# A decoder step on one core: fp32r products whose moving columns come in turn from two halves

## The chip, the core and the metric

The kernel runs on one core of a Trainium2 chip. The metric is the device time of one execution in microseconds (us), lower is better. Five engines matter: TensorE (PE in the profile; PEld is its weight load), VectorE (DVE), ScalarE (ACT), GpSimd (POOL) and SyncE (SP), which issues most transfers. Products are written into PSUM; only DVE and ACT read PSUM here.

## What is computed

One layer of a hybrid decoder trunk and a final norm, for a prompt of 1024 tokens and 8 sample tokens that share the weights. In the reference, cut to what matters:

```python
def layer(x, ...):
    h = rmsnorm(x, g_mix)
    u = h @ w_in                                  # 1024 -> 512 (pool) + 512 (value) + 512 (gate)
    glu = val * sigmoid(gate)
    ya = pool_mixer(concat(pool_hist, a), ...)    # windows 2/4/8/16, per-group 128x128 map
    yb = conv_mixer(concat(conv_hist, glu), ...)  # depthwise conv of width 31, LayerNorm, swish
    x = x + concat(ya, yb) @ w_out
    x = x + cross_attn(rmsnorm(x, g_attn), mk, mv, w_q, w_o)   # 4 heads, 256 memory tokens
    h = rmsnorm(x, g_ffn)
    x = x + (silu(h @ w_gate) * (h @ w_up)) @ w_down           # 2816 hidden channels
    return x

y = rmsnorm(layer(x), g_final)
```

The memory's keys and values (`mem_kv`) and the new pool and conv states are outputs too.

## The kernel before

**Layout.** Channels lie on the 128 partitions, tokens along the free dimension: T = 1032 columns, first the 512 even prompt tokens, then the 512 odd ones, then the 8 samples. Each product of an fp32 weight and an fp32 activation is made of three fp32r products: both factors are split into a rounded part and a rest, and `PASSES` gives the three pairs (rounded x rounded, rounded x rest, rest x rounded). All accumulate into the same PSUM columns. For every such matmul a 128x128 weight tile is loaded, and the moving operand is a contiguous run of columns: 344 (a third of T, `CW`) for the projections, 256 for keys and scores, 512 for values and attention outputs, 512 or 260 (half of 520, `TW`) in the gated and down parts. Before the change moving columns are read in the order in which they lie, and written to PSUM in the same order.

**Readers of PSUM.** DVE and ACT read a finished product once or twice: to scale it, add it to a residual, take an exponential, or split it again. Helpers `ch3`, `halves` and `as_banks` bring the SBUF side into the shape of the PSUM side (three banks of 344, two of 260).

**Stages,** in order of time: input projection with conv and pool windows (up to about 180 us), memory keys and values, output projection (to 297), queries, scores, softmax and attention values, mixed with the sample tokens' own attention, which DVE sums from caches that arrive by transfer (297 to 449), attention's output projection (449 to 540), then the gated part (22 hidden tiles, 540 to about 970; each from tile 2 on is `seven(f)`: seven products in the manner of Strassen and Winograd over blocks A11, A12, A22, S1 to S4), the down projection (`down(u)`, to 1138) and its last tiles with the final norm (`last_down`, `final`).

**What sets the order.** The body of the kernel only lists tasks: `add({"PE": pe(CW, 9)}, emit, reads, writes)`. `Program.order` plays them through as a list scheduler, with a price in us for each engine that may take the task, and emits each engine's instructions in the order that this play gives; where two engines are allowed ("DVE" or "Pool"), the one that would end sooner gets it. `pe(n, count)` is the price of `count` fp32r matmuls of `n` columns. The prices set the order and the engine alone; on the chip semaphores decide when a task runs.

Of the kernel before, what the change touches and what calls it, by code (L numbers as in the profile page):

```python
# [10 lines left out]
AF = mybir.ActivationFunctionType  # L11
# [250 lines left out]
def hybrid_step_kernel(ctx: ExitStack, tc: tile.TileContext, io):  # L262
# [228 lines left out]
    def step3(ps, w, wkeys, cols, x, k, first, last, spans=range(NCH), keys=None):  # L491


        def emit(e):
            for p, (wi, xi) in enumerate(PASSES):
                for c in spans:
                    e.matmul(ps[:, c, :CW], w[:, wi, cols], x[:, xi, c * CW : (c + 1) * CW],  # L497
                             start=first and p == 0, stop=last and p == 2)
# [234 lines left out]
    def gate_out(j, ps):  # L733
        t = scr(f"t{j}")
        tk = (t,)
        if j == 0:
            add({"ACT": act(T, True)}, lambda e: e.activation(ch3(t[:]), ps[:, :, :CW], AF.Copy), all3(ps), [tk])
# [7 lines left out]
    def value_out(j, ps, t):  # L745
# [4 lines left out]
        if j == 0:  # L750
            add({"DVE": dve(T), "ACT": act(T, True)}, lambda e: (
                e.activation(ch3(gb[:, i]), ps[:, :, :CW], AF.Copy) if e is nc.scalar else
                e.tensor_copy(ch3(gb[:, i]), ps[:, :, :CW])), all3(ps), [gk])
            add({"DVE": dve(T), "Pool": pool_tt(T)}, lambda e: e.tensor_tensor(gb[:, i], gb[:, i], t[:], ALU.mult), [gk, (t,)], [gk], lock=True)
        else:
            add({"DVE": dve(T)}, lambda e: e.tensor_tensor(ch3(gb[:, i]), ps[:, :, :CW], ch3(t[:]), ALU.mult), all3(ps) + [(t,)], [gk])
# [102 lines left out]
    def mixer_in(g):  # L859
        ps = group("w_in", xop)  # L860
        ab, ai = a2[g // 2], g % 2
        add({"DVE": dve(T)}, lambda e: e.tensor_tensor(ch3(ab[:, ai]), ps[:, :, :CW], ch3(Rx[:]), ALU.mult), all3(ps) + RX, [(ab, ai)])
# [6 lines left out]
    def keys(q):  # L869
        ps = mm_buf(f"kps{q}", 1)  # L870
        for i in range(2):
            w, wkeys = w_take("w_k")
            for k in range(KT):
                def emit(e, k=k, i=i, w=w):
                    for p, (wi, xi) in enumerate(PASSES):
                        e.matmul(ps[:, 0, i * NMEM : (i + 1) * NMEM], w[:, wi, block_cols(k)], memg[k // 4][:, xi, k % 4],  # L876
# [4 lines left out]
            kf[:], ps[:, 0].rearrange("p (i m) -> p i m", i=2), Rm().unsqueeze(1).to_broadcast([P, 2, NMEM]), ALU.mult),  # L881
# [62 lines left out]
    def values(c):  # L944
        ps = mm_buf(f"vps{c}", 2)
        for kk in range(4):
            w, wkeys = w_take("w_v")
            for k in (2 * kk, 2 * kk + 1):
                def emit(e, k=k, w=w):
                    col = (k % 2) * 512  # L950
                    for p, (wi, xi) in enumerate(PASSES):
                        for m in range(2):
                            e.matmul(ps[:, m], memg[k // 4][:, xi, k % 4, m * P : (m + 1) * P], w[:, wi, col : col + 512],  # L953
# [3 lines left out]
        for m in range(2):  # L957
            add({"ACT": act(512, True, 1)}, lambda e, m=m: e.activation(
                vf[:, m], ps[:, m], AF.Copy, scale=rmc[:, 2 * m : 2 * m + 1]), [(ps,), ("rmc",)], [(vf, m)])
# [7 lines left out]
    def out_a(n):  # L967
# [8 lines left out]
        add({"DVE": dve(T)}, lambda e: e.tensor_tensor(ch3(x1[j][:, i]), ps[:, :, :CW], ch3(x1[j][:, i]), ALU.add),  # L976
# [6 lines left out]
    def out_b(n):  # L983
# [8 lines left out]
        add({"DVE": dve(T)}, lambda e: e.tensor_tensor(ch3(x1[j][:, i]), ps[:, :, :CW], ch3(x1[j][:, i]), ALU.add), all3(ps) + [xk], [xk])  # L992
# [886 lines left out]
```

## Time and profile before

| | |
|---|---|
| median of 3 runs | 1219.57 us (1217.78 to 1220.19) |
| span of the profiled execution | 1217.6 us |
| TensorE busy | 1202.0 us, 99% of the span, 7736 matmul records |
| weight loads (PEld) busy | 1125.9 us, 92% |
| DVE, ACT, POOL busy | 931.2, 524.8, 250.1 us |
| mean granted TensorE clock | 0.997 |

The page lists no other time for the profiled execution than its span; it is set against the median of the runs here. TensorE is busy nearly throughout, but "busy" says only that some matmul was in flight: what one matmul takes has to be read from runs of equal matmuls that follow each other without a wait. A row of the lines by form gives line, engine, operation, output and inputs, shape, count, then busy us, mean ns of one from its start to its end (which is more than its distance to the next, since matmuls overlap), and idle time before it.

### The profile page before, as it was taken

What the parts mean: (1) busy time and instruction counts of PE and PEld (TensorE: products, weight loads), DVE (VectorE), ACT (ScalarE), POOL (GpSimd) and SP (SyncE); (2) the same over time, 40 slices, a digit from 0 to 9 for tenths busy, and PEclk for the clock granted to TensorE, in tenths of its full rate; (3) what the DMA queues carried; (4) which work ended last, traced back from release to release, by engine and by line L of the source; (5) the groups of instructions that cost most, each with busy time, mean ns of one, the idle gap of its engine ahead of it and who ended that gap; (6) DMA issues with size and microseconds to landing.
All of it is one profiled execution on the core that took longest, in us unless ns stands there. A gap on an engine that the chain in (4) does not pass through costs nothing.

```text
span 1217.6 us, 19433 instructions
## 1 busy us (share of the span) xinstructions
PE 1202.0 (99%) x7736; PEld 1125.9 (92%) x7736; DVE 931.2 (76%) x1548; ACT 524.8 (43%) x718; POOL 250.1 (21%) x297
## 2 busy tenths in 40 slices
PE   9999999999999999999999999999999999999997
PEld 9999988999999979999999999999999999999886
DVE  7899999766258886679877787777867798879754
ACT  7765656455135633454222322233222355544533
POOL 3568842231110102131000000000000024332101
PEclk9999999999999999999999999999999999999998
DMA  7334676326386774421332233222313597678612
GB/s 289 82 77 111 145 213 214 125 105 205 112 263 202 238 272 156 122 87 62 122 113 80 96 114 108 109 80 97 123 70 105 207 310 210 180 185 224 149 51 89
DMA packets 60170, 179.69 MB, mean 148 GB/s; under 512 B 7792, under 2 KB 11568, under 8 KB 58800
## 3 DMA queue, kind: packets, MB, share of 16 engines
q1 hardware_dynamic: 53392, 157.56, 37.1%
q0 software_dynamic: 6256, 20.54, 9.7%
q8 instruction: 60, 0.98, 0.3%
q10 hardware_dynamic: 432, 0.36, 0.1%
q14 instruction: 30, 0.25, 0.1%
HBM read 144.66 MB, written 33.78 MB: 147 GB/s over the span
## 4 chain that ended last, share of the span: by engine, by line
PE 78%; DVE 4%; DMA 1%; issue 1%; ACT 0%; POOL 0%; DVEq 0%; SPq 0%; POOLq 0%; ACTq 0%
PE pr L1355 47%; PE po L497 7%; PE fd L1698 6%; PE ps L497 5%; PE oa L497 4%; PE ob L497 4%; PE sc L1052 1%; DVE spcache_k L1149 1%; PE vps L953 1%; PE pv L1110 1%; DMA sbcache_v<-pd 1%; PE kps L876 0%; PE pmap L896 0%; DMA spcache_k<-in_cache_k 0%; DMA pd<-prow 0%
## 5 line engine op out<-in xcount | busy, mean ns | idle before, releaser
L1355 PEld LDWEIGHTS pr<-ab,wTb 128*128 128x128 f32 x1056 | 131.8, 188 | 3.5
L1355 PE MATMUL pr<-ab,wTa 128*128 128x260 f32 x1056 | 133.6, 282 | 0.2 <-DVE su L1371 0.2
L1355 PE MATMUL pr<-ab,wTb 128*128 128x260 f32 x1056 | 133.0, 282 | 0.0
L1355 PEld LDWEIGHTS pr<-ab,wTa 128*128 128x128 f32 x1056 | 130.8, 188 | 2.4 <-DVE su L1371 0.4
L1355 PE MATMUL pr<-ab,wG 128*128 128x512 f32 x528 | 129.2, 393 | 0.0
L1371 DVE TENSOR_TENSOR su<-pr,su 128x520 f32<-128x520 f32 (+1 forms) x112 | 77.7, 695 | 57.6 <-PE pr L1355 57.4
L1355 PEld LDWEIGHTS pr<-ab,wG 128*128 128x128 f32 x528 | 96.3, 188 | 19.7 <-DVE wG L396 0.4
L497 PE MATMUL ps<-xop,w 128*128 128x344 f32 x720 | 114.1, 320 | 0.0
L497 PEld LDWEIGHTS ps<-xop,w 128*128 128x128 f32 x720 | 113.6, 188 | 0.0
L1355 PEld LDWEIGHTS pr<-hb,dV 128*128 128x128 f32 x768 | 98.8, 188 | 4.1
L1355 PE MATMUL pr<-hb,dV 128*128 128x260 f32 x768 | 100.1, 283 | 0.0
L497 PE MATMUL ps<-xq,w 128*128 128x344 f32 x576 | 94.9, 322 | 0.1
L497 PEld LDWEIGHTS po<-oo,w 128*128 128x128 f32 x576 | 90.8, 188 | 0.6 <-DVE oo L1115 0.4
L497 PE MATMUL po<-oo,w 128*128 128x344 f32 x576 | 91.3, 320 | 0.0
L497 PEld LDWEIGHTS ps<-xq,w 128*128 128x128 f32 x576 | 90.8, 188 | 0.4 <-DMA w<-in_w_q 0.4
L710 DVE SCALAR_TENSOR_TENSOR cacc<-glu,vec,cacc 128x511 f32<-128x511 f32 (+14 forms) x116 | 76.9, 740 | 0.0
L1355 PE MATMUL pr<-hb,dW 128*128 128x512 f32 x288 | 74.5, 394 | 0.1
L385 ACT ACTIVATE w<-raw 128x1024 fp32r<-128x1024 f32 (+1 forms) x37 | 35.0, 950 | 86.7 <-PE po L497 24.4
L1698 PE MATMUL fd<-ho,w 128*128 128x260 f32 (+1 forms) x432 | 69.1, 321 | 0.0
L1698 PEld LDWEIGHTS fd<-ho,w 128*128 128x128 f32 x432 | 62.0, 188 | 6.9 <-issue 0.5
L1382 POOL MEMSET su<- 128x16 f32 x22 | 2.5, 113 | 318.9 <-PE pr L1355 267.7
L1355 PE MATMUL pr<-ab,wU 128*128 128x512 f32 x264 | 64.6, 393 | 0.0
(311 smaller groups left out, 2195.7 us busy)
## 6 DMA issues: line engine op xcount, KB each, us to landing
gr<-in_w_gu SPq DMA_DIRECT2D x44, 512.0 KB, 3.4
hb<-su SPq DMA_DIRECT2D x8, 1040.0 KB, 4.6
hs<-hb SPq DMA_DIRECT2D x16, 520.0 KB, 5.3
dr<-in_w_dn SPq DMA_DIRECT2D x16, 512.0 KB, 4.4
spcache_k<-in_cache_k SPq DMA_DIRECT2D x12, 512.0 KB, 5.7
hs<-hb SPq DMA_DIRECT2D x12, 512.0 KB, 4.6
raw<-in_w_in SPq DMA_DIRECT2D x10, 512.0 KB, 3.3
hb<-he SPq DMA_DIRECT2D x8, 520.0 KB, 2.8
```

Of the source, the lines that this page charges most:

```text
L385: e.activation(dst(0), src(), AF.Copy, scale=1.0 if gain is None else gain)
L497: e.matmul(ps[:, c, :CW], w[:, wi, cols], x[:, xi, c * CW : (c + 1) * CW], start=first and p == 0, stop=last and p == 2)
L710: e.scalar_tensor_tensor(acc[h][:, n:], src[:, : HALF - n], w, acc[h][:, n:], ALU.mult, ALU.add)
L953: e.matmul(ps[:, m], memg[k // 4][:, xi, k % 4, m * P : (m + 1) * P], w[:, wi, col : col + 512], start=(k == 0 and p == 0), stop=(k == KT ...
L1052: e.matmul(bank()[:, i * NMEM : (i + 1) * NMEM], qop[2 * h + dt][:, qi, tt * P : (tt + 1) * P], kk[:, ki, 2 * (h % 2) + dt], start=(dt == ...
L1110: e.matmul(ps[:, c], v[:, vi, m, col : col + P], pT[h][m][:, pi, sl], start=(m == 0 and p == 0), stop=(m == 1 and p == 2))
L1149: e.scalar_tensor_tensor(piece[:, b], piece[:, b], 1.0, bc[:, b], ALU.mult, ALU.mult, accum_out=out(m)[:, first + b : first + b + 1])
L1355: e.matmul(bank(c), w[:, wi, cols(j)], xs[0](j, xi)[:, c * n : (c + 1) * n], start=onto is None and j == 0 and p == 0, stop=j == nj - 1 an ...
L1371: from_sums(sums, "DVE", dve, lambda e, src, sl: e.tensor_tensor(as_banks(o(sl), src), src, as_banks(a(sl), src), op), [akey], [okey])
L1382: add({"Pool": 0.12}, lambda e: e.memset(o(), 0.0), [], keys)
L1698: e.matmul(view(i), w[:, wi, col : col + P], hops[k][:, xi, half, lo - half * HALF + i * width // count : lo - half * HALF + (i + 1) * wid ...
```

## The change

Three things change together.

1. Every fp32r matmul reads its moving columns in turn from two halves of the run: with n columns, first column 0, then n/2, then 1, then n/2 + 1 (`turns`). The output is written to PSUM in that order, one column after the other (`placed` only gives it the same shape). So PSUM column 2i holds column i of the first half and column 2i + 1 column i of the second. Plain fp32 products and transposes keep their order.
2. Every reader of such a PSUM result takes every second column (`drawn`): first the even places, then the odd ones, and writes or pairs them with contiguous SBUF halves. The shapes gain a dimension of 2; the number of elements stays. The maximum over a row of scores needs no order and is left as it is.
3. The planner's price of a matmul, `pe`, goes from 0.0135 + 0.000417 n us to the larger of 0.1125 and 0.0027 + 0.000417 n. For 260, 344 and 512 columns that is 0.1219 to 0.1125, 0.1570 to 0.1461 and 0.2270 to 0.2162 us.

```diff
+    def turns(ap):
+        return ap.rearrange("p (h n) -> p n h", h=2)
+    def placed(ap):
+        return ap.rearrange("p (n h) -> p n h", h=2)
+    def drawn(ap):
+        return ap.rearrange("p (n h) -> p h n" if len(ap.shape) == 2 else "p c (n h) -> p c h n", h=2)
+    def drawn3(ps):
+        return drawn(ps[:, :, :CW])
+    def ch3h(ap):
+        return ap.rearrange("p (c h n) -> p c h n", c=NCH, h=2)
...
     def pe(n, count=1):
-        return (0.0135 + 0.000417 * n) * count
+        return max(0.1125, 0.0027 + 0.000417 * n) * count
...
-                    e.matmul(ps[:, c, :CW], w[:, wi, cols], x[:, xi, c * CW : (c + 1) * CW],
+                    e.matmul(placed(ps[:, c, :CW]), w[:, wi, cols], turns(x[:, xi, c * CW : (c + 1) * CW]),
...
-            add({"DVE": dve(T)}, lambda e: e.tensor_tensor(ch3(t[:]), ps[:, :, :CW], ch3(Rx[:]), ALU.mult), all3(ps) + RX, [tk])
+            add({"DVE": dve(T)}, lambda e: e.tensor_tensor(ch3h(t[:]), drawn3(ps), ch3h(Rx[:]), ALU.mult), all3(ps) + RX, [tk])
...
-                e.activation(pr[:, tt], bank()[:, i * NMEM : (i + 1) * NMEM], AF.Exp, bias=st[:, 2 + i : 3 + i],
+                e.activation(halves(pr[:, tt]), drawn(bank()[:, i * NMEM : (i + 1) * NMEM]), AF.Exp, bias=st[:, 2 + i : 3 + i],
...
     def as_banks(ap, src):
-        return ap if len(src.shape) == 2 else ap.rearrange("p (c n) -> p c n", c=2)
+        return halves(ap) if len(src.shape) == 3 else ap.rearrange("p (c h n) -> p c h n", c=2, h=2)
...
-                        e.matmul(bank(c), w[:, wi, cols(j)], xs[0](j, xi)[:, c * n : (c + 1) * n],
+                        e.matmul(placed(bank(c)), w[:, wi, cols(j)], turns(xs[0](j, xi)[:, c * n : (c + 1) * n]),
...
-            add({engine: cost(sl.stop - sl.start)}, lambda e, src=src, sl=sl: emit(e, src(), sl), [key] + r, w)
+            add({engine: cost(sl.stop - sl.start)}, lambda e, src=src, sl=sl: emit(e, drawn(src()), sl), [key] + r, w)
```

The keys, values, scores, attention outputs, residual sums and last tiles are edited in the same manner. Line numbers of the changed kernel are 15 higher from here on.

The new price also moves work. First listing: POOL in the stage of conv and pool windows (`win` is a window sum of one channel group, a row with 511 or 512 columns its first step; `kT` the rest part of the keys; `w` weights). Before:

```order
L843 COPY win_1648<-a_531 128x1
L844 TENSOR_TENSOR win_1648<-a_531 128x511
L845 TENSOR_TENSOR win_1648<-a_531 128x512
L396 TENSOR_TENSOR kT_1656<-kf_1639,kT_1656 128x512
L840 COPY win_1648<-win_1648 128x2x2
L841 TENSOR_TENSOR win_1648<-win_1648 128x2x510
L396 TENSOR_TENSOR kT_1656<-kf_1711,kT_1656 128x512
```

And with the change, from the second group on:

```order
L858 COPY win_1839<-a_1421 128x1
L859 TENSOR_TENSOR win_1839<-a_1421 128x511
L860 TENSOR_TENSOR win_1839<-a_1421 128x512
L411 TENSOR_TENSOR kT_1844<-kf_1837,kT_1844 128x512
L855 COPY win_1839<-win_1839 128x2
L856 TENSOR_TENSOR win_1839<-win_1839 128x2x511
L858 COPY win_1886<-a_531 128x1
L859 TENSOR_TENSOR win_1886<-a_531 128x511
L860 TENSOR_TENSOR win_1886<-a_531 128x512
L855 COPY win_1886<-win_1886 128x2
L856 TENSOR_TENSOR win_1886<-win_1886 128x2x511
```

Before, POOL took the first step of one group out of four and DVE the other three; now POOL takes three of them and DVE one, and one more of the second and one more of the third steps.

Second listing: TensorE in the gated part, from one hidden tile to the next (`wG`, `wU`, `wTa`, `wTb` are the tile's weight blocks, `ab` the blocks of the activations; a product is two rows). Before:

```order
L1355 MATMUL pr_5851<-ab_0_4718,wTa_5762 128x260 x12
L1355 MATMUL pr_5851<-ab_1_5207,wTa_5762 128x260 x12
L1355 MATMUL pr_5931<-ab_0_4739,wU_5797 128x512 x6
L1355 MATMUL pr_5931<-ab_1_5214,wU_5797 128x512 x6
L1355 MATMUL pr_5851<-ab_0_4651,wTb_5793 128x260 x12
L1355 MATMUL pr_5851<-ab_1_5036,wTb_5793 128x260 x12
L1355 MATMUL pr_5983<-ab_0_4631,wG_5926 128x512 x6
L1355 MATMUL pr_5983<-ab_1_4946,wG_5926 128x512 x6
```

With the change:

```order
L1371 MATMUL pr_5802<-ab_1_5165,wG_5737 128x512 x6
L1371 MATMUL pr_5899<-ab_0_4725,wU_5786 128x512 x6
L1371 MATMUL pr_5899<-ab_1_5213,wU_5786 128x512 x6
L1371 MATMUL pr_5817<-ab_0_4709,wTa_5788 128x260 x12
L1371 MATMUL pr_5817<-ab_1_5205,wTa_5788 128x260 x12
L1371 MATMUL pr_5951<-ab_0_4637,wG_5912 128x512 x6
L1371 MATMUL pr_5951<-ab_1_4952,wG_5912 128x512 x6
L1371 MATMUL pr_5817<-ab_0_4650,wTb_5796 128x260 x12
L1371 MATMUL pr_5817<-ab_1_5045,wTb_5796 128x260 x12
```

The next tile's first product with `wG` now stands ahead of the last product with `wTb` of the tile before it, and the product with `wU` ahead of the one with `wTa`. The products themselves and their number are the same.

More of the change, by code (lines that the diff above doesn't have):

```diff
@@ L975, in out_a @@
             step3(ps, w, wkeys, out_cols(i)(k), opa[k], k, k == 0, k == 3)
[L976 removed]
+        add({"DVE": dve(T)}, lambda e: e.tensor_tensor(ch3h(x1[j][:, i]), drawn3(ps), ch3h(x1[j][:, i]), ALU.add),
             all3(ps) + [(x1[j], i)], [(x1[j], i)])
@@ L1051, in emit @@
                     for p, (ki, qi) in enumerate(PASSES):
-                        e.matmul(bank()[:, i * NMEM : (i + 1) * NMEM], qop[2 * h + dt][:, qi, tt * P : (tt + 1) * P],
-                                 kk[:, ki, 2 * (h % 2) + dt], start=(dt == 0 and p == 0), stop=(dt == 1 and p == 2))
+                        e.matmul(placed(bank()[:, i * NMEM : (i + 1) * NMEM]), qop[2 * h + dt][:, qi, tt * P : (tt + 1) * P],
+                                 turns(kk[:, ki, 2 * (h % 2) + dt]), start=(dt == 0 and p == 0), stop=(dt == 1 and p == 2))
         o = 2 * (h % 2)
@@ L1697, in emit @@
                     for i in range(count):
-                        e.matmul(view(i), w[:, wi, col : col + P], hops[k][:, xi, half, lo - half * HALF + i * width // count : lo - half * HALF + (i + 1) * width // count],
+                        e.matmul(placed(view(i)), w[:, wi, col : col + P],
+                                 turns(hops[k][:, xi, half, lo - half * HALF + i * width // count : lo - half * HALF + (i + 1) * width // count]),
                                  start=(k == 0 and p == 0), stop=(k == 5 and p == 2))
```

37 lines of the change are left out of this document (19 added, 18 removed).

## The prediction

> **What bounds the kernel now.** I read the windows by stage first, because they put a stage's TensorE time and its rivals' beside each other (columns: PE, PEld, DVE, ACT and POOL busy with their counts, granted clock, DMA share, GB/s).
>
> ```profile
> 0.00:60.00 60.00, 57.45 (x332) 55.92 (x333) 48.35 (x64) 42.26 (x55) 28.03 (x60) 1.00 0.54 183
> 60.00:180.00 120.00, 119.49 (x763) 116.24 (x762) 116.67 (x184) 70.89 (x94) 85.77 (x69) 1.00 0.56 139
> 337.00:449.00 112.00, 108.89 (x703) 101.01 (x701) 85.87 (x310) 52.17 (x116) 9.70 (x20) 1.00 0.73 233
> 560.00:960.00 400.00, 400.00 (x2682) 369.03 (x2682) 305.43 (x428) 109.87 (x141) 4.24 (x29) 1.00 0.29 101
> 960.00:1033.00 73.00, 73.00 (x491) 67.40 (x490) 63.87 (x88) 41.18 (x55) 20.13 (x26) 1.00 0.84 265
> 1033.00:1138.00 105.00, 104.85 (x696) 96.39 (x695) 89.72 (x131) 49.06 (x57) 32.10 (x38) 1.00 0.74 192
> sum 1218.00, PE 1201.96 PEld 1125.93 DVE 931.20 ACT 524.80 POOL 250.14; mean PE 109.27 PEld 102.36 DVE 84.65 ACT 47.71 POOL 22.74
> ```
>
> TensorE has work in 1202 of 1218 us, at a granted clock of 1.00 in each of these windows. A busy TensorE need not run at its peak, so the next question is what one matmul costs in a dense run. The chain of waits in order of time (start, length, what) has unmixed runs:
>
> ```profile
> 196.19 5.76 PE kps L876 x48
> 185.77 5.56 PE vps L953 x24
> 251.62 45.43 PE ob L497 x288
> ```
>
> That is 5.76 / 48 = 120.0 ns for 256 columns, 45.43 / 288 = 157.7 ns for 344, 5.56 / 24 = 231.7 ns for 512. From 256 to 512 columns one more column costs 111.7 / 256 = 0.436 ns. Products in plain fp32, which the change leaves alone, give a yardstick (lines by form; after the bar busy us, mean ns of one):
>
> ```profile
> L785 PE MATMUL Rm_ps<-side,ones_d 128*128 128x256 f32 x2 | 0.6, 377 | 0.0
> L1729 PE MATMUL fin_ps<-fin,ones_d 128*128 128x512 f32 x2 | 1.0, 592 | 0.0
> L1007 PE MATMUL r_ps<-ones_d,xss 128*128 128x2 f32 x16 | 1.8, 246 | 0.0
> ```
>
> They stream a column in (592 - 377) / 256 = 0.840 ns, twice 0.420. If an fp32r column needs half of that, 256, 344 and 512 columns need 107.5, 144.5 and 215.0 ns, and **12.5, 13.2 and 16.7 ns of each matmul are excess**, part fixed and part growing with the columns. The third row bounds the other side: with two columns to stream and a new weight tile each, a matmul takes 1.8 / 16 = 112 ns. That is what loading 128x128 weights costs, and no 256- or 260-column matmul gets below it. So the excess is all that the change can win: it leaves the count of matmuls and columns as it was.
>
> **The change, part by part.**
>
> *Reading in turn (the moving operand).* Whether alternate reads remove the excess no row shows, since every moving operand of before is contiguous. The excess shows only where columns are taken at the full rate, and its slope (0.436 against 0.420) grows with the columns: it looks like the supply of columns, not like the array, and the read order acts on the supply. I take the full removal, down to the floor of 112.5 ns at 256 and 260 columns, and to the streaming time plus 2 ns or so (an estimate: the new price allows 2.7) at 344 and 512: 147 and 217 ns. The counts (lines by form):
>
> ```profile
> L1355 PE MATMUL pr<-ab,wTa 128*128 128x260 f32 x1056 | 133.6, 282 | 0.2 <-DVE su L1371 0.2
> L1355 PE MATMUL pr<-ab,wTb 128*128 128x260 f32 x1056 | 133.0, 282 | 0.0
> L1355 PE MATMUL pr<-hb,dV 128*128 128x260 f32 x768 | 100.1, 283 | 0.0
> L1698 PE MATMUL fd<-ho,w 128*128 128x260 f32 x288 | 35.7, 285 | 0.0
> L1355 PE MATMUL pr<-ab,wG 128*128 128x512 f32 x528 | 129.2, 393 | 0.0
> L1355 PE MATMUL pr<-hb,dW 128*128 128x512 f32 x288 | 74.5, 394 | 0.1
> L1355 PE MATMUL pr<-ab,wU 128*128 128x512 f32 x264 | 64.6, 393 | 0.0
> L1698 PE MATMUL fd<-ho,w 128*128 128x512 f32 x144 | 33.6, 394 | 0.0
> L497 PE MATMUL ps<-xop,w 128*128 128x344 f32 x720 | 114.1, 320 | 0.0
> L497 PE MATMUL ps<-xq,w 128*128 128x344 f32 x576 | 94.9, 322 | 0.1
> L497 PE MATMUL po<-oo,w 128*128 128x344 f32 x576 | 91.3, 320 | 0.0
> L497 PE MATMUL oa<-opa,w 128*128 128x344 f32 x288 | 46.6, 322 | 0.0
> L497 PE MATMUL ob<-opb,w 128*128 128x344 f32 x288 | 45.6, 320 | 0.0
> L1052 PE MATMUL sc<-kT,qo 128*128 128x256 f32 x192 | 25.6, 284 | 0.3 <-ACT probs L1069 0.3
> L876 PE MATMUL kps<-memg,w 128*128 128x256 f32 x192 | 23.5, 283 | 0.0
> L953 PE MATMUL vps<-w,memg 128*128 128x512 f32 x96 | 23.5, 400 | 0.0
> ```
>
> At 260 columns stand 3168 and at 256 384: 3552 x 7.5 ns = 26.6 us. At 344 stand 2448: x 10.7 = 26.2 us. At 512 stand 1320: x 14.7 = 19.4 us. Together 72 us; groups under 100 instructions with the same forms (psg, psv, pv) add some 3: **75 us, 6.2% of TensorE's 1202**. The bounds: with no fixed part and no floor, 10.8, 13.2 and 16.7 ns would go, 38 + 32 + 22 = 92 us; on the other side nothing goes, or the reads get slower (rivals).
>
> *A rule beside these rows.* The Trainium skill, TensorE: Matmul & The Clock Gate, section "Wait — 56ns, not 53.3ns?", says that back-to-back matmuls start N / 2.4 GHz plus about 2.5 ns apart. This case's contiguous rows disagree (231.7 ns where it gives 215.8); by it the excess is no property of the array, and at 344 and 512 columns it would save 12 and 16 ns where I count 10.7 and 14.7.
>
> *Every second column (the PSUM readers).* DVE's and ACT's reads step over 8 bytes where they stepped over 4. No row has such a step in PSUM. The nearest (lines by form):
>
> ```profile
> L1371 DVE TENSOR_TENSOR pp<-pr,pp 128x520 f32<-128x520 f32 x28 | 19.5, 695 | 5.8 <-PE pr L1355 5.4
> L1379 DVE TENSOR_TENSOR su<-su,Rf 128x520 f32<-128x520 f32 x44 | 30.6, 696 | 5.1 <-ACT su L1407 4.7
> L1706 DVE TENSOR_TENSOR x<-fd,x 128x260 f32<-128x260 f32 x16 | 6.6, 425 | 12.7 <-PE fd L1698 12.6
> ```
>
> An element costs (695 - 425) / 260 = 1.04 ns, and it is the same from PSUM as from SBUF (695, 696), so the source doesn't set the pace. I take no cost; the upper bound is a doubling, 0.54 us for each read of 520 (a rival).
>
> *The planner's price* lowers 260 columns from 121.9 to 112.5 ns, 344 from 157 to 146, 512 from 227 to 216, and the work is dealt out anew. In the conv and window stage POOL takes over pieces from DVE (first listing above): two first steps of 511 + 512 elements, 1.4 us each at DVE's 1.04 ns and fixed part, and two later ones of about 1.2 us. Some 5 us leave DVE. In the gated stage the next tile's first product goes ahead of the last one of the tile before (second listing): the same matmuls, and DVE's read of that last product comes 12 x 217 ns = 2.6 us later. DVE is at 305 of 400 us there and has room. I cost both at nothing; if POOL is late with a window, TensorE waits for the map's product behind it, a few us.
>
> *What of the 75 us lands.* A stage saves its TensorE time x 6.2%, unless another engine is next.
> - 560 to 960: 400 us fall to 375, DVE needs 305. All 25 land.
> - 60 to 180: 7.4 us would leave 112.6, and DVE needs 116.7 less 5, so it is as full as TensorE. I take 5.
> - 337 to 449: the chain leaves TensorE here:
>
> ```profile
> 346.55 4.46 DMA pd<-prow
> 351.08 6.49 DMA sbcache_v<-pd
> 360.53 5.54 DVE spcache_k L1149 x32
> ```
>
> Transfers and sums of the sample group set the pace in part, and no matmul price shortens them. Of 6.8 us I take half.
> - 0 to 60: inputs still arrive, PE is busy 57 of 60. Of 3.6 us I take 2.
> - 960 to 1138: DVE's 153.6 us fit into 178 - 11 = 167, but the DMA share of 0.84 becomes 0.90. Of 11 us I take 9.5.
>
> Left out are 2.4 + 3.4 + 1.6 + 1.5, about 9 us: **66 us land**. The profiled execution spans 1217.6 us and the median of the runs is 1219.57, so 2 us lie around the span or between runs. 1219.6 - 66 = 1153 us.
>
> **The rivals.**
>
> *B, part of the excess stays.* If only the part that grows with the columns went (0.016 ns x 260, 344, 512 = 4, 5.5, 8 ns), TensorE would save 14 + 14 + 11 = 39 us, of which some 34 land: 1185. For it: the excess of 12.5 ns at 256 is mostly fixed, and may belong to the change of weights.
>
> *C, the read order does nothing.* TensorE keeps 120, 158 and 232 ns, and the planner now believes in matmuls that end sooner. In the gated stage nobody waits for that; in the first 180 us POOL gets 10 us more work. 1217 to 1228, taken as 1221.
>
> *D, the stepped PSUM reads double.* In 960 to 1138 the 104 reads (44, 32 and 28 by line 1371) cost 56 us more: DVE needs 209 of 178 us, and that stage loses 31 us in place of winning 9.5. In the gated stage some 60 us more make 365 of the 375 left. 66 - 41 and a little elsewhere: about 1200. Against it speak 695 and 696 ns.
>
> *E, alternate reads starve TensorE: the slower side.* Two neighbouring fp32 columns may come from SBUF in one access at the full rate; taken in turn from places 512 to 1024 bytes apart (half of 256 to 512 columns of 4 bytes), each would need its own. The price is at most the fp32 pace, 0.840 ns a column: 218, 289 and 430 ns, 98 + 131 + 198 ns more, and with the counts 348 + 321 + 261 = 930 us: some 2150 us. It decides from 0.436 ns a column on, since any slower column adds to every matmul in a stream that fills 1202 of 1218 us. For it: the excess at the full rate says that the supply is near its limit. Against it: near that limit contiguous columns lose only 0.016 of 0.436 ns, though a weight load runs beside every matmul (1126 us of loads in the sum row).
> The Trainium skill, Advanced Engine Details and Errata, section "Memory Cachelines", speaks for E: SBUF lines hold 16 bytes, at least two accesses in a row should hit one line, and another line each time is penalised. No run here shows it yet.
>
> **How the numbers follow.** Full removal has 0.62: 1153, its own range 1130 (nearly all of the 92 us) to 1175 (two thirds of the 66). B 0.10, C 0.08, D 0.05, E 0.15. I put E above C because a supply at its limit that is asked for other lines answers one way or the other. Range: full removal, B, D and half or more of C make about 0.8: 1130 to 1228. A measurement of this kernel tells about 0.2% (2.4 us) from no change. Faster: 0.62 + 0.10 + 0.05 = 0.77. Within: half of C, 0.04. Slower: E and the rest of C, 0.19.
>
> **What would show it.** The runs ob, vps and kps in the chain: 147, 217 and 112.5 ns each if right; 158, 232, 120 under C; over 200 at 260 columns under E. The 520-column reads of line 1371 stay at 695 ns, or D shows as 1236. The gated stage lasts 375 us for 2682 matmuls, with DVE still at 305. If 60 to 180 shrinks by less than 5 us with DVE at its end, the early stage was mis-sized; if 337 to 449 keeps its length, the sample group's transfers ate the gain.

## The result, and the profile after

The changed kernel takes **1179.99 us** (median of 4 runs, 1177.33 to 1181.42) beside 1219.88 us (1217.78 to 1222.16, 4 runs) for the kernel before on the same chip: a ratio of **0.968 (95% interval 0.966 to 0.970)**. The forecast was 1153 us in a range of 1130 to 1228. It is faster, as forecast, but by 40 us and not by 66.

First what went as predicted: the matmuls. These rows are from the changed kernel's lines by form (after the bar: busy us, mean ns of one from start to end; the busy time over the count is a little above the distance between matmuls, since a group's tails count too).

```profile
L1371 PE MATMUL pr<-ab,wTa 128*128 128x260 f32 x1056 | 125.1, 275 | 0.0
L1714 PE MATMUL fd<-ho,w 128*128 128x512 f32 x144 | 31.2, 379 | 0.0
L891 PE MATMUL kps<-memg,w 128*128 128x256 f32 x192 | 22.2, 276 | 0.9 <-DMA w<-in_w_k 0.9
L969 PE MATMUL vps<-w,memg 128*128 128x512 f32 x96 | 24.4, 412 | 8.4 <-POOL w L411 8.4
L1023 PE MATMUL r_ps<-ones_d,xss 128*128 128x2 f32 x16 | 1.8, 246 | 0.0
```

The 1056 matmuls with `wTa`, at 260 columns, fall from 133.6 to 125.1 us, the 144 of `fd` at 512 columns from 33.6 to 31.2 us (233 to 217 ns each). The group among these that got slower, vps (23.5 to 24.4 us), names the trouble: TensorE waited 8.4 us ahead of it. The dense runs in the chain of waits (start, length, what) give the distances without tails:

```profile
202.11 5.36 PE kps L891 x48
207.47 18.38 PE oa L512 x126
```

5.36 / 48 = 111.7 ns at 256 columns and 18.38 / 126 = 145.9 ns at 344. From start to next start, the median over the whole trace is 112, 146 and 216 ns for 256 and 260, 344 and 512 columns, where it was 120, 157 and 231.

Second the stages (columns as in the windows of before):

```profile
0.00:60.00 60.00, 57.66 (x363) 56.13 (x364) 48.15 (x63) 44.28 (x57) 27.87 (x59) 1.00 0.59 198
60.00:180.00 120.00, 112.81 (x749) 108.29 (x748) 116.11 (x179) 66.44 (x87) 83.15 (x70) 0.99 0.54 134
180.00:210.00 30.00, 21.62 (x114) 18.37 (x114) 27.29 (x34) 14.68 (x17) 14.44 (x12) 0.83 0.48 145
339.00:453.00 114.00, 103.92 (x705) 97.81 (x703) 84.41 (x305) 51.91 (x117) 11.68 (x25) 0.99 0.70 232
550.00:950.00 400.00, 400.00 (x2874) 379.64 (x2873) 326.58 (x463) 126.27 (x167) 8.15 (x36) 1.00 0.34 116
```

From 550 to 950 us TensorE never stops and does 2874 matmuls in 400 us, where before it did 2682. From 60 to 180 us, where before it was busy 119.5 of 120 us with 763 matmuls, it is now busy 112.8 with 749: it does not get more done, it waits. Between 180 and 210 us it is busy 21.6 of 30.

Third, where the 42 us between the two spans (1217.6 and 1175.6) came from. The view of one tile gives the start of its first and last instruction. `po`, attention's output projection, ends the first half of the kernel. Its row in the trace of before, and in that of the changed kernel:

```profile
L497 PE MATMUL po<-oo,w x576: 314/319/427, 449.1 to 540.0; 128*128 128x344 f32 x192
```

```profile
L512 PE MATMUL po<-oo,w x576: 308/309/413, 453.8 to 539.4; 128*128 128x344 f32 x192
```

**The first half takes 539.4 us instead of 540.0, so it gained nothing. All of the gain lies behind it: 677.6 us became 636.2.** The matmuls behind `po` (3168 of 260 columns by 8 ns, 1224 of 512 by 15) save 43.7 us, and 41.4 landed. Those ahead of it (2592 of 344 columns by 11 ns, 384 of 256 by 8, 192 of 512 by 15) save 34.5 us, and 0.6 landed. The waits of TensorE (us in total, times, longest) show gaps that were not there before. The longest single wait in the trace of before, and then the first four rows of the changed kernel:

```profile
PE psg L497 <- ACT w L385: 1.5, 1, 1.5
```

```profile
PE vps L969 <- POOL w L411: 8.4, 1, 8.4
PE ps L512 <- DMA w<-in_w_in: 3.5, 1, 3.5
PE sc L1068 <- DVE sm L1089: 3.1, 1, 3.1
PE ob L512 <- DVE opb L411: 2.7, 1, 2.7
```

The timeline of POOL in the changed kernel (start, length, what, and idle time before it) shows what stands ahead of the piece of weights that vps waits for:

```profile
174.20 1.28 POOL L411 TENSOR_TENSOR kT<-kf,kT 128x512 fp32r<-128x512 f32 x1 [7.90 <-ACT kT L400]
...
179.99 1.26 POOL L859 TENSOR_TENSOR win<-a 128x511 f32<-128x511 f32 x1
181.22 1.26 POOL L860 TENSOR_TENSOR win<-a 128x512 f32<-128x512 f32 x1
182.54 0.19 POOL L855 COPY win<-win 128x2 f32<-128x2 f32 x1
182.68 1.89 POOL L856 TENSOR_TENSOR win<-win 128x1022 f32<-128x1022 f32 x1
184.64 0.19 POOL L855 COPY win<-win 128x4 f32<-128x4 f32 x1
184.78 1.88 POOL L856 TENSOR_TENSOR win<-win 128x1020 f32<-128x1020 f32 x1
186.62 2.35 POOL L411 TENSOR_TENSOR w<-raw,w 128x1024 fp32r<-128x1024 f32 x1
```

These are the window steps that the new prices gave to POOL, and the weights' rest part stands behind them on the same engine; vps starts at 189.02, when it has ended. Whether that is the cause or only where a lateness comes to light is what the experiments had to tell.

### The profile page after: what moved, and what is told of

Same layout as the page of the kernel before. It is cut to its first block, busy times and chain, and to the rows that moved or that the text cites. A ratio compares the mean times of both kernels' runs of the same rounds, so it can differ in the third digit from the quotient of the medians.

```text
span 1175.6 us, 19448 instructions
## 1 busy us (share of the span) xinstructions
PE 1130.2 (96%) x7736; PEld 1074.0 (91%) x7736; DVE 928.1 (79%) x1538; ACT 517.1 (44%) x712; POOL 257.7 (22%) x313
## 4 chain that ended last, share of the span: by engine, by line
PE 71%; DVE 14%; DMA 6%; issue 4%; ACT 2%; POOL 2%; DVEq 0%; SPq 0%; POOLq 0%; ACTq 0%
PE pr L1371 45%; PE ps L512 5%; PE po L512 5%; PE fd L1714 4%; DVE cacc L725 4%; PE ob L512 4%; PE oa L512 3%; DMA spcache_k<-in_cache_k 1%; DVE spcache_v L1165 1%; DMA raw<-in_w_v 1%; PE vps L969 1%; DMA dr<-in_w_dn 1%; DMA w<-in_w_q 1%; PE pv L1126 1%; DVE spcache_k L1165 1%
## 5 line engine op out<-in xcount | busy, mean ns | idle before, releaser
L1371 PE MATMUL pr<-ab,wTa 128*128 128x260 f32 x1056 | 125.1, 275 | 0.0
L1371 PEld LDWEIGHTS pr<-ab,wTa 128*128 128x128 f32 x1056 | 123.6, 190 | 1.6
L1371 PEld LDWEIGHTS pr<-ab,wTb 128*128 128x128 f32 x1056 | 122.7, 190 | 1.5
L1371 PE MATMUL pr<-ab,wTb 128*128 128x260 f32 x1056 | 123.6, 275 | 0.0
L1371 PE MATMUL pr<-ab,wG 128*128 128x512 f32 x528 | 121.8, 380 | 0.6 <-POOL wG L411 0.6
L512 PE MATMUL ps<-xop,w 128*128 128x344 f32 x720 | 105.8, 310 | 3.5 <-DMA w<-in_w_in 3.5
L512 PEld LDWEIGHTS ps<-xop,w 128*128 128x128 f32 x720 | 105.0, 189 | 3.8 <-DMA w<-in_w_in 3.8
L512 PE MATMUL ps<-xq,w 128*128 128x344 f32 x576 | 87.7, 311 | 1.7 <-DMA w<-in_w_q 1.7
L512 PEld LDWEIGHTS po<-oo,w 128*128 128x128 f32 x576 | 84.0, 189 | 2.2 <-POOL w L411 1.3
L400 ACT ACTIVATE w<-raw 128x1024 fp32r<-128x1024 f32 (+1 forms) x35 | 32.9, 942 | 85.8 <-PE po L512 23.5
L400 ACT ACTIVATE wG<-gr 128x1024 fp32r<-128x1024 f32 x22 | 23.3, 1058 | 91.0 <-PE pr L1371 85.8
```

The source lines that it names most:

```text
L400: e.activation(dst(0), src(), AF.Copy, scale=1.0 if gain is None else gain)
L512: e.matmul(placed(ps[:, c, :CW]), w[:, wi, cols], turns(x[:, xi, c * CW : (c + 1) * CW]), start=first and p == 0, stop=last and p == 2)
L1371: e.matmul(placed(bank(c)), w[:, wi, cols(j)], turns(xs[0](j, xi)[:, c * n : (c + 1) * n]), start=onto is None and j == 0 and p == 0, stop ...
```

## The experiments

There are two questions: where did the gain of the first half go, and what about the read order makes a matmul faster or slower. Theory P on the first: the price's new order costs the missing time. Theory Q: the order is harmless, and the time goes to something else.

### The two parts apart

The changed kernel with the old price, which gives every engine the instruction order that it had before:

```diff
-        return max(0.1125, 0.0027 + 0.000417 * n) * count
+        return (0.0135 + 0.000417 * n) * count
```

> The change with the planner's price of before put back: the order of instructions on every engine is that of before, the reads in turn and the stepped PSUM reads stay. Theory P (the new deal of work is what lost part of the gain: POOL, given two more window steps, hands over a w_v block late, and TensorE waits 8.4 us for it): the time falls below the change's, 1160 to 1173 us, and the keys' products end before 202 us (they end at 202 before and at 207 with the change). Rival Q (DVE's conv sums bound the first 200 us whatever the plan, 116.7 of 120 us busy before): the time stays within 4 us of the change's 1180, and TensorE waits as long as with the change in the first 210 us, for others. Both expect matmuls 112, 146 and 216 ns apart, since the reads set them and not the order.

Measured: 1166.13 us (1158.16 to 1167.23), ratio 0.957 (0.954 to 0.960). And the kernel before with the new price alone (order as in the changed kernel, reads as before):

```diff
-        return (0.0135 + 0.000417 * n) * count
+        return max(0.1125, 0.0027 + 0.000417 * n) * count
```

> The kernel before with the new price alone: the order of the change, contiguous reads. Both theories expect matmuls 120, 157 and 231 ns apart as before. P: the new order costs time by itself, 1225 to 1235 us, with a wait of vps for POOL. Q: the new order is nearly free at the old speed, 1217 to 1223 us, because TensorE is then the bound and covers POOL's lateness.

Measured: 1246.87 us (1244.03 to 1248.07), ratio 1.024 (1.022 to 1.026), worse than either theory had it. Here are the `po` rows of the two, the first from the changed kernel with the old price, the second from the kernel before with the new one:

```profile
L512 PE MATMUL po<-oo,w x576: 309/309/413, 439.4 to 523.8; 128*128 128x344 f32 x192
```

```profile
L497 PE MATMUL po<-oo,w x576: 314/319/428, 476.1 to 568.4; 128*128 128x344 f32 x192
```

With their spans (1165.4 and 1246.2 us) the four kernels make a table of the time up to the end of `po` and behind it:

| us, up to / behind | old reads | new reads |
|---|---|---|
| old order | 540.0 / 677.6 | 523.8 / 641.6 |
| new order | 568.4 / 677.8 | 539.4 / 636.2 |

The new order costs 28.4 us in the first half with the old reads and 15.6 with the new; behind it, it costs nothing or wins 5. The reads win 16 to 29 us in the first half and 36 to 42 behind it. So the reads alone won 67 us in the new order (1246.9 - 1180.0) and 51 in the old one, where 66 were forecast for the whole, and the price took 14 us (new reads) to 30 us (old ones) away. P stands, Q falls. The wait on POOL's weights is there in the kernel before too, once it has the new order (its waits of TensorE):

```profile
PE vps L953 <- POOL w L396: 8.3, 1, 8.3
PE ob L497 <- DVE opb L396: 3.4, 1, 3.4
PE sc L1052 <- DVE sm L1073: 2.7, 1, 2.7
```

The same three places wait as in the changed kernel, with the old reads and their slower matmuls. It is the order that makes them, not matmuls that outrun the other engines.

### What about the read order

Two more orders were tried at once. First, two neighbouring columns from each half in turn:

```diff
-        return ap.rearrange("p (h n) -> p n h", h=2)
+        return ap.rearrange("p (h n t) -> p n h t", h=2, t=2)
```

(with `placed` changed alike, as in all runs of this part).

> The change, with two neighbouring columns from one half and then two from the other. The products leave in another column order than the readers take, so the values differ; the work is the same. If each step to the neighbouring column costs (half of the steps are such now): 260, 344 and 512 columns stand halfway, about 116, 151 and 224 ns apart. If only the long run of neighbours costs: 112, 146 and 216 as with the change. If pairs serve the supply better or worse than single columns do: below 112 at no width (the floor), or above 120.

Then the even columns and after them the odd ones, so that each step is 8 bytes and every 16 bytes are visited twice, far apart in time:

```diff
-        return ap.rearrange("p (h n) -> p n h", h=2)
+        return ap.rearrange("p (n h) -> p h n", h=2)
```

> The change, with the even columns of the run first and then the odd ones: a step of 8 bytes and no turn between far places. The products leave in another column order than the readers take, so the values differ; the work is the same. If the turn between two far places is what removes the excess: 120, 157 and 231 ns or more. If any step away from the neighbouring column does it: 112, 146 and 216 ns. If a step of 8 bytes halves what an access brings in: up to 218, 289 and 430 ns.

Measured: 1704.81 and 2317.57 us (one execution each). The 512-column rows of the two, from the lines by form, and the 256-column row of the second:

```profile
L1714 PE MATMUL fd<-ho,w 128*128 128x512 f32 x144 | 47.4, 501 | 0.0
```

```profile
L1714 PE MATMUL fd<-ho,w 128*128 128x512 f32 x144 | 65.3, 646 | 0.0
L891 PE MATMUL kps<-memg,w 128*128 128x256 f32 x192 | 44.2, 409 | 0.0
```

Pairs in turn: 328 ns from start to start at 512 columns and 220 at 344. That is neither of the figures that were expected but the third branch, that pairs serve the supply worse. Evens, then odds: 453 ns at 512 and 228 at 256, which is 0.88 ns a column, twice the 0.436 of the natural order. So the read order can cost a factor of two; the danger that the prediction called E exists, only not for this order.

From these four orders came theory L: the stream has two readers, one for its first, third, fifth column and so on and one for the others, and each holds the 16 bytes (four columns) that it read last. What counts is how often each reader must fetch another 16 bytes. In natural order each uses two columns of a fetch and throws away two; from two halves each uses all four. It is measured against theory F: the columns have to come from places far apart. Two orders with near places tell them apart. Columns 0, 2, 1, 3 of each four (L: each reader still uses two columns of each fetch, as in natural order):

```diff
-        return ap.rearrange("p (h n) -> p n h", h=2)
+        return ap.rearrange("p (n h t) -> p n t h", h=2, t=2)
```

> The change, with the columns of each group of four in the order 0, 2, 1, 3: no neighbour follows its neighbour, but no far place is read. The products leave in another column order than the readers take, so the values differ; the work is the same. Theory L (two readers feed TensorE, one takes every first and one every second place of the stream; each holds one line of 16 bytes, four columns, and needs about 1.75 ns for the next one: 0.436 x 4 in natural order, 0.88 x 2 with evens then odds): each reader needs one line in four columns, as in natural order: 112 to 120, 157 and 231 ns for 260, 344 and 512 columns. Rival F (TensorE must draw from two far places, banks or halves): no faster than natural, and slower where neighbouring lines clash, up to 233, 306 and 453 ns.

And 0, 4, 1, 5, 2, 6, 3, 7 of each eight (L: each reader uses all four; widths that eight doesn't divide keep the halves):

```diff
-        return ap.rearrange("p (h n) -> p n h", h=2)
+        if ap.shape[1] % 8 == 0:
+            return ap.rearrange("p (n h t) -> p n t h", h=2, t=4)
+        return ap.rearrange("p (h n) -> p n h", h=2)
```

> The change, with groups of eight in the order 0, 4, 1, 5, 2, 6, 3, 7 where eight divides the columns (256, 344, 512); 260 columns stay in turn from two halves. The products leave in another column order than the readers take, so the values differ; the work is the same. Theory L: each reader goes through one line of four columns before it needs the next, one in eight columns: 112, 146 and 216 ns, as with far halves. Rival F: the two lines are neighbours, so the excess stays or grows: 120 or more, 157 or more, 231 or more.

Measured: 1245.73 and 1177.77 us (one execution each). The 512- and 256-column rows of the first, then of the second:

```profile
L1714 PE MATMUL fd<-ho,w 128*128 128x512 f32 x144 | 33.6, 394 | 0.0
L891 PE MATMUL kps<-memg,w 128*128 128x256 f32 x192 | 23.4, 283 | 0.0
```

```profile
L1718 PE MATMUL fd<-ho,w 128*128 128x512 f32 x144 | 31.2, 379 | 0.0
L895 PE MATMUL kps<-memg,w 128*128 128x256 f32 x192 | 22.2, 275 | 0.1
```

The first is the natural order's row to the digit (33.6, 394; 283), and its time is that of the old reads with the new price, 1246.9. The second is the row of the halves (31.2, 379). F falls: the neighbouring eight columns do as well as two halves. L foretold both.

A last order takes columns in turn from four quarters:

```diff
-        return ap.rearrange("p (h n) -> p n h", h=2)
+        return ap.rearrange("p (h n) -> p n h", h=4)
```

> The change, in turn from four quarters instead of two halves. The products leave in another column order than the readers take, so the values differ; the work is the same. Theory L: each reader alternates between two quarters and needs another line for each of its columns, one in two columns of the stream: 0.63 (as pairs in turn) to 0.88 ns a column, 169 to 233, 220 to 306 and 328 to 453 ns. Rival F: four far places are no worse than two: 112, 146 and 216 ns.

Measured: 1383.89 us (one execution). Three rows of the lines by form:

```profile
L1714 PE MATMUL fd<-ho,w 128*128 128x512 f32 x144 | 40.3, 443 | 0.0
L1714 PE MATMUL fd<-ho,w 128*128 128x260 f32 x288 | 35.6, 284 | 0.0
L891 PE MATMUL kps<-memg,w 128*128 128x256 f32 x192 | 27.8, 308 | 0.0
```

It is slower than halves at every width, as L says and F does not: 280 ns from start to start at 512 columns, 185 at 344, 143 at 256. But L's price was a fetch for each column, and that would have been 328 to 453 ns at 512. And 260 columns take 121 ns, hardly more than the natural order's 120 (35.6 us here against 35.7 before), while 256 columns take 143. In which places of memory the quarters of 260 columns lie, against those of 256, may matter; no run here shows it. So of L this much is shown at 256, 344 and 512 columns: the two orders in which every second column of the stream walks through whole runs of four are the fastest of the seven tried. Its price for a stream that misses each time is wrong (0.88 ns a column with evens then odds, 0.629 from 256 to 512 columns with pairs, 0.535 with quarters), and that there are two readers is inferred from the pattern, not shown.

The Trainium skill, Advanced Engine Details and Errata, section "Memory Cachelines", says that SBUF lines hold 16 bytes and at least two accesses in a row should hit one line. Evens then odds (two hits in a row on each line, half the pace) and the halves (no two columns in a row from one line, the best pace of all) both disagree with it as it reads for one stream. Counted over every second column it fits: four hits in the halves (216 ns at 512 columns), two in natural order (231), one in evens then odds (453). Pairs in turn (328) and quarters (280) would also have one hit and are faster than evens then odds, so the count of hits alone doesn't set the price.

### The price where it does no harm

If the harm is all ahead of the gated part, the old price there and the new one behind it should beat both kernels. The planner's factors for the early part (`MARGINS["early"]`) hold up to the gated part, and there the instruction order of TensorE is now that of before.

```diff
     def pe(n, count=1):
+        if pg.margin is MARGINS["early"]:
+            return (0.0135 + 0.000417 * n) * count
         return max(0.1125, 0.0027 + 0.000417 * n) * count
```

> The change with the price of before for the tasks up to the gated part and the new price from there on: TensorE's order is that of before up to the gated part, and that of the change in what follows. If the order of the first 540 us is what the new price spoils and the later part gains a little by it (TensorE lost 7.4 us to waits in the down part with the old price, 2.5 with the new): the attention's output projection ends at 524 us as with the old price, and the time is 1158 to 1164 us. If the loss is spread over the whole: 1166 to 1175 us.

Measured: **1155.02 us** (1152.53 to 1156.61), ratio **0.949 (0.947 to 0.950)**. It beats both, and is 62.6 us below the kernel before (1217.6 us beside it), where 66 were forecast. The span is 1153.3 us; its `po` row, and one window:

```profile
L514 PE MATMUL po<-oo,w x576: 309/309/413, 432.3 to 516.6; 128*128 128x344 f32 x192
```

```profile
60.00:180.00 120.00, 113.99 (x764) 109.69 (x764) 117.27 (x188) 72.81 (x96) 84.17 (x68) 1.00 0.56 137
```

The first half ends at 516.6 us, 22.8 before the changed kernel's; behind it stand 636.7 us, as in the changed kernel (636.2). Against the old price throughout it gains 11 us by the medians and 12.1 between the two profiled executions. Of these 4.9 lie behind `po` (641.6 to 636.7), where the orders differ. The other 7.2 lie ahead of it, where all engines have the same order: so much can differ between two executions of that half (from 210 to 300 us the granted clock is 0.96 with the old price throughout and 1.00 with the mixed one), and so much is not to be read into a difference. From 60 to 180 us DVE is busy 117.3 of 120 us and TensorE 114.0: DVE is the fuller of the two, the limit that the prediction gave this stage.

### What in the new order costs

The first 210 us as one window, of before, of the changed kernel and of the mixed price:

```profile
0.00:210.00 210.00, 206.85 (x1257) 197.94 (x1257) 194.58 (x285) 135.16 (x173) 122.12 (x132) 1.00 0.56 159
```

```profile
0.00:210.00 210.00, 192.09 (x1223) 182.78 (x1224) 191.55 (x274) 125.40 (x161) 125.45 (x139) 0.97 0.55 154
```

```profile
0.00:210.00 210.00, 198.03 (x1286) 187.88 (x1286) 197.72 (x290) 135.95 (x174) 120.89 (x133) 1.00 0.59 166
```

With the new price DVE has started 11 to 16 instructions fewer by then and ACT 12 to 13 (125.4 us of work against 135.2 and 136.0), and POOL 6 to 7 more: it is behind, and leans on POOL.

Up to the end of `po` TensorE is busy 505.6 us in the changed kernel and 498.6 with the mixed price, for the same matmuls. So of the 22.8 us between the two 15.8 are waits and 7.0 are matmuls that take longer; of the 28.4 us with the old reads, 22.8 are waits and 5.6 longer matmuls (539.4 us busy against 533.8). The longer matmuls go with the clock: over that stretch the granted clock is 0.98 in both kernels with the new order and 1.00 in the two others. Four runs tried to name what makes the waits.

The piece of weights that vps waits for, kept away from POOL:

```diff
-    def split(dst, key, src, n, r, gain=None, ps=False):
+    def split(dst, key, src, n, r, gain=None, ps=False, pool=True):
...
-        if gain is None and not ps and not state.get("alone"):
+        if gain is None and not ps and pool and not state.get("alone"):
...
+            split(lambda p: w[:, p], lambda p: (w, p), lambda: raw[:], 1024, [(raw,)], pool=name != "w_v")
```

> The change, with the rest part of the w_v blocks not open to POOL (DVE makes it); the order of TensorE and DVE before that point is the change's. If POOL's late w_v block is what costs 8.4 us: no wait of vps for POOL, the keys' products end at 199 us or earlier (207 with the change), the time is 1169 to 1174 us. If POOL was late because all of that stage is late (its input waited for ACT and DVE): another wait takes its place, the keys' products end at 203 us or later, 1176 to 1181 us.

Measured: 1182.70 us (1179.88 to 1185.09), ratio 0.971 (0.969 to 0.973): nothing gained. Its waits of TensorE, and what DVE did ahead of the window's last step that TensorE waited for:

```profile
PE pmap L912 <- DVE win L869: 10.7, 1, 10.7
```

```profile
175.62 14.35 DVE L725 SCALAR_TENSOR_TENSOR cacc<-glu,vec,cacc 128x508 f32<-128x508 f32 x22
```

The wait has gone to the next piece in line, behind 22 convolution sums on DVE, and is longer. The 8.4 us behind POOL's queue were where the lateness came to light; taking that piece off POOL, and giving it to DVE, did not remove the lateness.

The windows on DVE alone, so that POOL has none:

```diff
-            add({"Pool": pool_tt(SEQ) + 0.1, "DVE": dve(SEQ) + 0.08}, emit, [ck], [nk], lock=True)
+            add({"DVE": dve(SEQ) + 0.08}, emit, [ck], [nk], lock=True)
```

> The change, with the window sums open to DVE alone; TensorE's order differs from the change's by six moved rows. POOL's w_v block then stands ahead of everything that waited for windows. If the windows on POOL are what made the stage up to 207 us late: the keys' products end at 199 us or earlier, no wait of over 3 us before them, 1168 to 1173 us. If DVE, which had room for nothing more in that stage (116.1 of 120 us between 60 and 180 us with the change), only takes the lateness over: they end at 204 us or later, 1176 to 1184 us.

Measured: 1181.78 us (1177.61 to 1185.41), ratio 0.970 (0.967 to 0.973). The waits of TensorE again move:

```profile
PE oa L512 <- DVE kf L895: 7.3, 1, 7.3
PE pmap L912 <- DVE win L869: 6.4, 2, 4.1
```

DVE takes the lateness over. Taking the windows off POOL wins nothing back; but it gives more to DVE, which was nearly full, so that this run alone doesn't clear them.

That left the belief itself: with the new price and the early factor of 0.93 the planner counts a 344-column matmul as 136 ns, and it takes 146. Two runs make it count more. The mixed price with the early part raised to 157 ns:

```diff
-            return (0.0135 + 0.000417 * n) * count
+            return 1.075 * (0.0135 + 0.000417 * n) * count
```

> Mixed prices as before, the early price raised by 7.5%: with the planner's early factor of 0.93 it believes in 157 ns for 344 columns, where the chip takes 146 (with the change's price it believes in 136, with the price of before in 146). If the loss comes from believing in matmuls that are faster than the chip's: waits in the first 540 us no more than with mixed prices (30 us), 1148 to 1157 us. If the early order is good only at the price for which its list of pieces was arranged, and any other price spoils it: 1162 to 1185 us.

Measured: 1179.10 us (1178.08 to 1180.48), ratio 0.968 (0.967 to 0.970); `po` ends at 540.9 us. And the changed kernel with TensorE's early factor at 1.0, so that it counts 146 ns, the true one:

```diff
-    "early": {"PE": (0.93, 0.0), "DVE": (0.93, 0.0), "Pool": (1.0, 0.0), "ACT": (1.0, 0.0)},
+    "early": {"PE": (1.0, 0.0), "DVE": (0.93, 0.0), "Pool": (1.0, 0.0), "ACT": (1.0, 0.0)},
```

> The change with the planner's early factor for TensorE at 1.0 in place of 0.93: it believes in 146.2, 216.2 and 112.5 ns, what the chip takes, and within 0.2 ns at 344 columns and 5 ns at 512 of what mixed prices make it believe. If the belief in the right speed is what matters: within 4 us of mixed prices, 1151 to 1159 us. If the order hangs on small differences of price: 8 us or more away from them, most likely above, 1163 to 1180 us.

Measured: 1168.55 us (1168.13 to 1172.61), ratio 0.960 (0.959 to 0.962); `po` ends at 529.4 us. Counting 136 ns gives 1180, counting 146 by the old price with its factor 1155, 146 by the new price without it 1168.6, and 157 gives 1179. A belief that is too short can be a part of the cause: the true one by the new price wins back some 10 of the 24 us. It isn't all of it, since one that is too long loses as much, and two prices that put 256 and 344 columns within 1 ns of each other, and 512 by 5 ns apart (211 and 216), differ by 13.5 us (the factor also raises the few plain fp32 products of that part). **The order hangs on small differences of price**, and which single move of it costs the time isn't settled.

## Why the prediction was right, and where it was wrong

**The reading term: right.** 112, 146 and 216 ns were measured where 112.5, 147 and 217 were taken. With the counts that the prediction lists, 3552 x 8 + 2448 x 11 + 1320 x 15 = 75 us, where it had 72; with psg, psv and pv (144 more of 344 columns, 96 of 512) 78, where it had 75. The floor from the plain row with two columns (112 ns, again 1.8 us for 16 after) held to the nanosecond. B, which left the fixed part in place, and C fall by that. The rule that the prediction set beside the rows, the Trainium skill's TensorE: Matmul & The Clock Gate, section "Wait — 56ns, not 53.3ns?", gives 215.7 ns at 512 columns; these traces agree once the columns come in turn (216) and not in natural order (231).

**Stepped reads of PSUM: right.** Two rows of the changed kernel's DVE, by form, then one of its ACT with the same row before:

```profile
L1387 DVE TENSOR_TENSOR pp<-pr,pp 128x520 f32<-128x520 f32 x28 | 19.4, 693 | 3.4 <-PE pr L1371 3.3
L1723 DVE TENSOR_TENSOR x<-fd,x 128x260 f32<-128x260 f32 x16 | 6.6, 425 | 10.3 <-PE fd L1714 6.5 <-DMA out_yT<-x 3.7
```

```profile
L1391 ACT ACTIVATE su<-pr 128x512 f32<-128x512 f32 x24 | 14.2, 594 | 54.4 <-PE pr L1371 54.4
```

```profile
L1375 ACT ACTIVATE su<-pr 128x512 f32<-128x512 f32 x24 | 14.2, 592 | 12.6 <-PE pr L1355 12.0
```

693 and 425 ns, where 695 and 425 stood before; ACT's 594 ns were 592. D falls.

**E: the mechanism exists, but not for this order.** It argued that each column taken in turn needs an access of its own. With evens then odds the pace was indeed 0.88 ns a column, a little above E's price (228 to 453 ns where it gave 218 to 430). But from two halves each of the two streams of columns walks through neighbours, and the pace was the best of all: by theory L, which fits but isn't proven, an access is then shared by a stream's neighbours. The argument looked at columns that follow each other; the orders tried say that every second one has to be looked at.

**The gated stage: right.** 375 us were predicted for its 2682 matmuls with DVE still at 305. The window after does 2874 in 400 us: 2682 take 373 us, and DVE's 326.6 by the same factor is 304.8. In all that stands behind `po`, 41.4 of 43.7 us landed; the prediction had set aside 1.5 us there, for the down projection.

**The new deal: wrong.** The step that failed is "I cost both at nothing; if POOL is late with a window, TensorE waits for the map's product behind it, a few us." The new order costs 28 us with the old reads and 16 to 23 with the new ones in the first half (539.4 against 523.8 and 516.6). Of the two moves that it looked at, nothing was near the truth for the gated products: behind `po` the order costs nothing. For the window pieces it isn't settled: taking them off POOL won nothing back, but loaded DVE. But the price stands in every TensorE task, the whole first half was dealt out anew, and two moves were priced in its place. Without that loss the forecast of 66 us comes near: with the mixed price 62.6 us landed, with the old price throughout 51. The list of what would show it did name the symptom (a stage of 60 to 180 us that shrinks by less than 5), yet took DVE's fullness for its reason. The sample group's stage, from the last `ob` to the last `pv`, took 152.0 us before (296.7 to 448.7), 151.1 after and 145.6 with the mixed price. Its matmuls (576 of 344 columns, 192 of 256, 96 of 512) save 9.3 us: with the mixed price 6.4 landed, so that 2.9 were lost where the prediction set 3.4 aside; in the changed kernel 0.9 landed, 5.5 less.

**The number: inside the range, but not for the reason given.** 1180 us lies outside the range that full removal had by itself (1130 to 1175), although the removal was full. It lies inside the stated one because that was widened for B, D and C, and it is nearest to B's 1185, whose mechanism the rows refute. A full removal and a loss that was put at nothing happen to add up to it: in that the hit was luck.

## What to carry to other kernels

An fp32r matmul whose columns are read in natural order loses 8 to 15 ns (6 to 7%); read in turn from two halves, or as 0, 4, 1, 5, 2, 6, 3, 7, it doesn't, and DVE and ACT take the interleaved result for nothing, but other orders cost up to double, so a read order is measured before it is used. When a price in a planner changes together with the code, the two are timed apart: a truer price made the order worse by 14 to 30 us here, and keeping the old one where it had served gave the best kernel. A wait in the profile that names an engine is tested by taking the named piece away before it is believed: here the wait moved to the next piece and the time stayed.

## What had not been expected of the hardware

- The order in which a moving operand's columns are read changes an fp32r matmul at 512 columns from 216 ns (two halves, or by four within eight) over 231 (natural, and 0, 2, 1, 3 just the same), 280 (four quarters) and 328 (pairs in turn) to 453 (evens, then odds).
- With four quarters 260 columns take 121 ns and 256 columns 143: the narrower product is the slower one. No run here tells why.
- After the 8.4 us in which TensorE had no work, its granted clock is 0.83 from 180 to 210 us and 0.50 from 189 to 194, when it works again; the kernel before has 1.00 in every window shown. Most of the first eight matmuls behind the wait (512 columns) start 427 ns apart, where 216 is their usual distance: here a wait cost more than its own length. With the mixed price, whose longest wait up to the end of `po` is 2.1 us, the clock is 1.00 all that time. That it is the wait which lowers the clock is read from their order in time; no run tests it alone. The vps group, of which 32 of 96 matmuls run behind the wait, is busy 24.4 us with a mean of 412 ns. These are the first eight in the timeline (start, length), and the group's row with the mixed price, 2.3 us less for the same 96 matmuls:

```profile
189.02 3.78 PE L969 MATMUL vps<-w,memg 128*128 128x512 f32 x8 [8.38 <-POOL w L411]
```

```profile
L971 PE MATMUL vps<-w,memg 128*128 128x512 f32 x96 | 22.1, 386 | 0.9 <-DVE kf L897 0.9
```
